# Batched matmul: y loaded four batches at a time with 24 KB runs, x transposed in blocks on VectorE, products on four row tiles

## The chip, the cores and the metric

One core of a Trainium2 chip. The metric is the device time of one execution in microseconds (us), lower is better. Each execution is marked fast or slow; for one core, slow means over 1.5% above the fastest of the same kernel. Time ratios are computed as the mean time of one kernel's fast runs over that of the other's fast runs of the same rounds, so they are not quite the ratios of the medians that are quoted beside them.

## The reference

```python
batch, dim_i, dim_j, dim_k = 32, 256, 512, 384      # x: [32,256,512], y: [32,512,384], f32
def reference(x, y):
    return np.einsum('bij,bjk->bik', x, y).astype(np.float32)
```

x is 16.8 MB, y 25.2 MB, the result 12.6 MB: 54.5 MB have to move.

## The kernel before

x comes four batches per DMA: 32 partitions a batch, 8 rows (16 KB) a partition. y comes one batch per DMA, four rows (6,144 B) on each of 128 partitions. x is transposed on the tensor engine (PE) against an identity; the copies out of PSUM, the memory that PE writes its products to, round it to f16 and write single elements 8 bytes apart, so that the columns of the later product stand in the right order. The stages of different batches are interleaved: while batch s-1 is multiplied, batch s-2 is copied out and batch s is rounded.

```python
    def transpose(q):                                   # one group of four batches
        xt_of[q] = xt_pool.tile([P, Q, NJ, NI, PQ, Q], MM_DT, name="xt_sb")
        for t in range(NJ):
            for e in range(NI):
                t_ps = tpsum_pool.tile([P, Q, Q, PQ], F32, name="t_ps")
                for h in range(Q):
                    keep(nc.tensor.transpose(t_ps[:, h]..., x_sb[:, h * NI + e, t::NJ], identity))
                dst = xt_of[q][:, :, t, e].rearrange("c g p h -> c h g p")    # 8-byte steps
                ...                                     # DVE and ACT in turn: dst <- t_ps
    # [cut: load, round_y, multiply on 128 rows, collect, store]
    for s in range(B + 2):
        if s + ahead < B: load(s + ahead)
        if s >= 2:        collect(s - 2)
        if 1 <= s <= B:   multiply(s - 1)
        if s < B and s % Q == 0: transpose(s // Q)
        if s < B:         round_y(s)
        if s >= 2:        store(s - 2)
```

## Time and profile before

| | before |
|---|---|
| time at prediction, median of 3 | 136.56 us |
| time over 6 runs, median | 136.39 us |
| profiled span | 134.7 us |
| transfers, share of the span | 97.9% |
| busiest compute engine | PE, 66% |

In the profile PE is the tensor engine, DVE is VectorE and ACT is ScalarE; PEclk is the clock that PE was granted, in tenths of full speed. The page gives, for each engine, its busy time and share of the span; then the span in 40 slices with the busy share of each in tenths; then groups of instructions with busy time, mean ns of one, and the idle time before them with what ended it.

### The profile page before, as it was taken

The numbers are of one execution on the slowest core, as the hardware profiler recorded it, in microseconds if no ns is written. First come the engines' busy times: TensorE is split into PE (matmuls) and PEld (weight loads), VectorE is DVE, ScalarE is ACT, GpSimd is POOL, SyncE is SP. The second block draws the span as 40 slices with busy tenths as digits, with TensorE's granted clock in tenths as the row PEclk, the third lists the DMA queues.
The fourth block names the chain that finished last, engine by engine and source line by source line (L and its number), as shares of the span: only waits on it lengthen the run. The fifth ranks groups of instructions, "written<-read, shape, count | busy, mean of one in ns | idle before, by whom it ended". The sixth has DMA issues, their size and how long they took to land.

```text
span 134.7 us, 1539 instructions
## 1 busy us (share of the span) xinstructions
PE 89.5 (66%) x512; PEld 66.6 (49%) x512; DVE 73.7 (55%) x128; ACT 80.1 (59%) x129; POOL 0.7 (1%) x6
## 2 busy tenths in 40 slices
PE   0049499769677908949794983949459492794920
PEld 0048368644564408925492543936259360793510
DVE  0008855975397503873489340796228870378720
ACT  3007994996299602795479650699218990179910
POOL 2000000000000000000000000000000000000000
PEclk9999999999999985686999599599995999559995
DMA  5999999999999999999999999999999999999992
GB/s 131 399 413 423 447 412 416 416 434 414 404 422 451 425 399 424 421 435 437 400 416 430 438 425 410 421 418 454 407 409 425 433 440 402 421 421 413 412 410 84
DMA packets 10375, 54.62 MB, mean 405 GB/s; under 512 B 1152, under 2 KB 1152, under 8 KB 9344
## 3 DMA queue, kind: packets, MB, share of 16 engines
q1 hardware_dynamic: 10368, 54.53, 97.9%
q8 instruction: 4, 0.07, 0.2%
q14 instruction: 3, 0.02, 0.0%
HBM read 41.94 MB, written 12.58 MB: 405 GB/s over the span
## 4 chain that ended last, share of the span: by engine, by line
DMA 79%; PE 8%; ACT 5%; DVE 2%; issue 2%; SPq 1%; DVEq 0%
DMA y_sb<-in_y_dram 30%; DMA x_sb<-in_x_dram 27%; DMA out_dram<-o_sb 21%; PE o_ps L115 4%; PE t_ps L84 4%; ACT xt_sb L94 2%; ACT y_r L102 2%; DVE xt_sb L92 1%; DVE y_r L104 1%; DVE o_sb L130 0%; SPq L69 0%; ACT o_sb L128 0%; SPq L63 0%; DVEq L130 0%
## 5 line engine op out<-in xcount | busy, mean ns | idle before, releaser
L94 ACT CAST xt_sb<-t_ps 128x512 f16<-128x512 f32 x32 | 39.8, 1350 | 44.0 <-PE t_ps L84 43.9
L92 DVE CAST xt_sb<-t_ps 128x512 f16<-128x512 f32 x32 | 40.1, 1323 | 40.3 <-PE t_ps L84 40.2
L84 PE MATMUL t_ps<-identity,x_sb 128*128 128x128 f32 x256 | 43.4, 340 | 24.5 <-DMA x_sb<-in_x_dram 24.3
L115 PE MATMUL o_ps<-y_r,xt_sb 128*128 128x384 f16 x256 | 46.3, 342 | 14.9 <-ACT y_r L102 14.9
L84 PEld LDWEIGHTS t_ps<-identity,x_sb 128*128 128x128 f32 x256 | 41.1, 216 | 27.8 <-issue 26.4
L115 PEld LDWEIGHTS <-xt_sb 128*128 128x128 f16 x256 | 26.2, 102 | 34.2 <-issue 19.9
L102 ACT CAST y_r<-y_sb 128x384 f16<-128x384 f32 x64 | 30.2, 527 | 0.6 <-DMA y_sb<-in_y_dram 0.6
L130 DVE COPY o_sb<-o_ps 128x384 f32<-128x384 f32 x32 | 17.8, 556 | 15.1 <-PE o_ps L115 15.1
L104 DVE CAST y_r<-y_sb 128x384 f16<-128x384 f32 x64 | 19.9, 354 | 0.4 <-DMA y_sb<-in_y_dram 0.4
L128 ACT COPY o_sb<-o_ps 128x384 f32<-128x384 f32 x32 | 15.4, 483 | 3.8 <-PE o_ps L115 3.8
L94 ACT ACT_TABLE_LOAD x1 | 1.3, 1283 | 0.7 <-PEq L168 0.7
masks.py:199 POOL TENSOR_SCALAR_AFFINE_SELECT identity<-identity 128x128 f32<-128x128 f32 x1 | 0.3, 294 | 0.1
masks.py:197 POOL MEMSET identity<- 128x128 f32 x1 | 0.2, 205 | 0.3 <-POOLq L168 0.3
L168 POOL MEMSET const-bfloat16-1.0<- 128x1 bf16 x1 | 0.1, 102 | 0.0
L168 POOL MEMSET const-uint8-127<- 128x1 uint8 x1 | 0.1, 102 | 0.0
L168 POOL MEMSET const-float32-0.0<- 128x1 f32 x1 | 0.1, 99 | 0.2 <-issue 0.2
L168 POOL MEMSET const-float32-1.0<- 128x1 f32 x1 | 0.1, 99 | 0.0
## 6 DMA issues: line engine op xcount, KB each, us to landing
y_sb<-in_y_dram SPq DMA_DIRECT2D x32, 768.0 KB, 15.1
x_sb<-in_x_dram SPq DMA_DIRECT2D x8, 2048.0 KB, 14.2
out_dram<-o_sb SPq DMA_DIRECT2D x32, 384.0 KB, 14.1
```

The source lines that it names most:

```text
L84: nc.tensor.transpose(t_ps[:, h].rearrange("c g p -> c (g p)"), x_sb[:, h * NI + e, t::NJ], identity,)
L92: keep(nc.vector.tensor_copy(dst, t_ps))
L94: keep(nc.scalar.copy(dst, t_ps))
L102: keep(nc.scalar.copy(yr_of[b][:, t], y_sb[:, t]))
L104: keep(nc.vector.tensor_copy(yr_of[b][:, t], y_sb[:, t]))
L115: nc.tensor.matmul(ps_of[b][e], xt_sb[:, t, e].rearrange("c p h -> c (p h)"), y_r[:, t], start=(t == 0), stop=(t == NJ - 1),)
L128: keep(nc.scalar.copy(o_of[b][:, e], ps_of[b][e]))
L130: keep(nc.vector.tensor_copy(o_of[b][:, e], ps_of[b][e]))
L168: nc = _bacc.Bacc("TRN2", target_bir_lowering=False, num_devices=1)
```

## The change

The intent is fewer and longer DMA packets: y in one load for each of the 8 groups, with runs (adjacent bytes that make one packet) of 24,576 B (the last group in two halves of 12,288 B, so 9 loads). That puts each batch on 32 partitions, so a product contracts over 32 rows, and four batches can share the 128 rows of PE as row tiles. x needs only 32x32 blocks transposed, which VectorE (DVE) does, without PE or PSUM.

```diff
-LAG = 8
+LATE = 8
+LAST = 2
+ROUND = (1, 0, 1, 1, 0, 1, 0, 1)
+    def load_y(n):
+        src = y[n * Q : (n + 1) * Q].rearrange("g (p c) k -> (g p) c k", c=C)
+        w = C // (LAST if n == N - 1 else 1)
+        for c in range(0, C, w):
+            keep(nc.sync.dma_start(out=y_of[n][:, c : c + w], in_=src[:, c : c + w]))
+    def transpose_x(n):
+        xt_of[n] = xt_pool.tile([P, C, NE, S, H], MM_DT, name="xt_sb")
+        for h in range(H):
+            rows = slice(h * NE, (h + 1) * NE)
+            keep(nc.scalar.copy(xr[:, rows], x_sb[:, rows].rearrange("q r (j c) -> q r c j", c=C)))
+            for e in range(NE):
+                keep(nc.vector.transpose(xt_of[n][:, :, e, :, h], xr[:, h * NE + e]))
+    def multiply(n, y_r):                       # all 8 PSUM banks, all end with the last c
+        ps = [[psum_pool.tile([P, K], F32, name="o_ps") for e in range(NE)] for g in range(Q)]
+        for c in range(C):
+            for e in range(NE):
+                for g in range(Q):
+                    rows = slice(g * S, (g + 1) * S)
+                    keep(nc.tensor.matmul(ps[g][e], xt_sb[rows, c, e]..., y_r[rows, c], ...))
+    for n in range(N + 1):
+        if n + 1 < N: load_y(n + 1)
+        if n + 2 < N: load_x(n + 2)
+        if n < N:
+            transpose_x(n)
+            collect(n, multiply(n, round_y(n)))
+        ...                                     # stores of the group before
 # [cut: load_x, the rounding in eight pieces (5 DVE, 3 ACT), collect, pools]
```

## The prediction

> **What bounds the kernel now.** I read the page from the top: busy shares, slices, DMA queues, groups of instructions.
>
> ```profile
> span 134.7 us, 1539 instructions
> PE 89.5 (66%) x512; PEld 66.6 (49%) x512; DVE 73.7 (55%) x128; ACT 80.1 (59%) x129; POOL 0.7 (1%) x6
> ...
> PEclk9999999999999985686999599599995999559995
> DMA  5999999999999999999999999999999999999992
> ...
> q1 hardware_dynamic: 10368, 54.53, 97.9%
> ```
>
> No compute engine is above 66%, while the DMA row is full from the second slice to the last but one: the transfers bound the kernel. 97.9% of 134.7 us is 131.9 us of transfer; only 2.8 us of start and end are not. The chain of waits agrees: 79% of it is DMA. So there are two questions: how much transfer time the change saves, and whether the compute still hides behind it.
>
> The groups give the unit costs:
>
> ```profile
> L94 ACT CAST xt_sb<-t_ps 128x512 f16<-128x512 f32 x32 | 39.8, 1350 | 44.0 <-PE t_ps L84 43.9
> L92 DVE CAST xt_sb<-t_ps 128x512 f16<-128x512 f32 x32 | 40.1, 1323 | 40.3 <-PE t_ps L84 40.2
> ...
> L102 ACT CAST y_r<-y_sb 128x384 f16<-128x384 f32 x64 | 30.2, 527 | 0.6 <-DMA y_sb<-in_y_dram 0.6
> L130 DVE COPY o_sb<-o_ps 128x384 f32<-128x384 f32 x32 | 17.8, 556 | 15.1 <-PE o_ps L115 15.1
> L104 DVE CAST y_r<-y_sb 128x384 f16<-128x384 f32 x64 | 19.9, 354 | 0.4 <-DMA y_sb<-in_y_dram 0.4
> L128 ACT COPY o_sb<-o_ps 128x384 f32<-128x384 f32 x32 | 15.4, 483 | 3.8 <-PE o_ps L115 3.8
> ```
>
> The odd ones are the first two. A 384-column copy out of PSUM takes DVE 556 ns and ACT 483 ns; 512 columns should take about 690 and 590. They take 1323 and 1350, nearly the same on two engines that otherwise differ. Reading PSUM and rounding to f16 are each cheap in the other rows; what is special is the destination: single f16 elements 8 bytes apart. That write costs about (1300-150)/512 = 2.2 ns an element on either engine.
>
> The timeline of the first batches gives back-to-back costs and the first landing:
>
> ```profile
> 8.69 4.02 PE L84 MATMUL t_ps<-identity,x_sb 128*128 128x128 f32 x20 [8.69 <-DMA x_sb<-in_x_dram]
> ...
> 15.27 1.18 DVE L104 CAST y_r<-y_sb 128x384 f16<-128x384 f32 x4
> 15.88 1.81 ACT L102 CAST y_r<-y_sb 128x384 f16<-128x384 f32 x4
> 16.51 5.36 PE L115 MATMUL o_ps<-y_r,xt_sb 128*128 128x384 f16 x32 [1.90 <-ACT y_r L102]
> ...
> 22.38 2.50 DVE L92 CAST xt_sb<-t_ps 128x512 f16<-128x512 f32 x2 [1.21 <-PE t_ps L84]
> ```
>
> x lands at 8.7 us. Thirty-two products take 5.36 us: starts 162.5 ns apart at full clock. Two of the strided copies take 2.50 us, so the second starts some 1.15 us after the first: the slow write is throughput, not latency.
>
> **What the Trainium skill says.**
> - "DMA: Bandwidth & Descriptors", section "Why small descriptors are slow", has a fixed overhead per packet. The trace agrees: its packets of 3,072, 6,144 and 16,384 B take 121, 234 and 611 ns (medians), which is 8 ns plus 27.2 B per ns.
> - "SBUF — State Buffer", section "Specifications (TRN2)", gives 16-byte lines that need at least two hits for full bandwidth. The strided copies above hit each line twice (8-byte steps) and still take 2.2 ns an element, so for these writes the measurement is worse than the page. A read with 64-byte steps, which the change adds, hits each line once; this trace has none.
> - "VectorE: DVE Perf Modes", section "The three transpose paths", gives 311 ns for a 128x128 bf16 transpose in 32x32 blocks. At one element a cycle (the 556 ns copy has 1.04 ns an element) four times the columns would be an estimated 311+400 = 0.71 us. No run here has one.
> - "TensorE: Matmul & The Clock Gate", section "Part 3: Packing small matmuls — row/col tiling", measured 3.07 times the speed for four row tiles with 512 columns. No run here shows it yet.
>
> **The change, part by part.**
>
> Transfers. y goes from 4096 packets of 6,144 B to 1024 of 24,576 B. By the fit the new one takes 8+904 = 912 ns. Over 16 engines: 4096*234/16 = 59.9 us becomes 1024*912/16 = 58.4 us, so 1.5 us less. The number of DMAs falls from 72 to 49; the 1152 four-byte completion packets of 9 ns become 784, 0.2 us less. x and out keep their packets. In all 1.7 us of 134.7, or 1.3%: the most that can be won. The transfers then take some 130.2 us, 16.3 us per group of four batches.
>
> Removed compute: 256 transposes on PE (43.4 us busy) and 64 PSUM copies (79.9 us of DVE and ACT). None of it was on the bound.
>
> Added compute, per group, eight groups:
> - ACT: 4 roundings of x, 1024 elements, contiguous writes, reads 64 bytes apart. At ACT's 0.83 ns an element plus 0.15, 1.0 us each; if the reads pay as the strided writes do, 2.4 us each.
> - DVE: 8 block transposes of 512 f16, written 8 bytes apart, the same destination stride as the 1.3 us copies. At 2.2 ns an element: 1.15 us each back to back, 9.2 us. Without that price 0.71 us, 5.7 us.
> - Rounding y in eight pieces of 768. DVE has 0.30 us per 384 back to back, plus 0.20: 0.50*5 = 2.5 us. ACT 0.45+0.32 = 0.77*3 = 2.3 us. PE can start after the first, at 0.5 us.
> - PE: 128 products of 32 rows, in 32 sets of four row tiles. With the page's 3.07, 162.5*4/3.07 = 212 ns a set, 6.8 us (estimate). PE will have been idle for the transposes, and here idle stretches are followed by half clock (0.57 and 0.60 in stretches at 49 and 60 us, records of 3.4 or 6.8 us): 3.4 us for the first 8 sets, then 24*212 = 5.1 us: 8.5 us.
> - Eight PSUM copies, four each: 1.9 us.
>
> What matters is the order. Before, the stages of different batches were interleaved on each engine, and the products had four PSUM banks beside four for transposes. Now one group takes all eight banks, every accumulator ends with the last of 16 steps, and the order of instructions shows DVE doing 8 transposes, 5 roundings, 4 copies, then the next group's transposes; ACT likewise. Those 4 copies wait for PE, so the next group's transposes wait for PE too, and PE waits for the transposes. Nothing of one group overlaps the next except transfers. The period is therefore a sum:
>
> first ACT piece and transposes, (1.0+9.2 = 10.2 us with cheap reads; 4*2.4+2.3 = 11.9 us with dear ones), about 11 us; + 0.5; + 8.5; + 1.9 = 21.9 us.
>
> That is over the 16.3 us of transfers, so the bound passes from DMA to this loop. Sum: x lands 8.7; eight periods, 175; the last stores about 3 us: span 187 us. The timed median lies 1.9 us above the profiled span (136.56 against 134.7), giving 189 us.
>
> **Rivals.**
> 1. Transposes at one element a cycle and cheap reads: 1.0+5.7+0.5+8.5+1.9 = 17.6 us. Group 0 must wait for y until about 16 us and ends at 27; 7*17.6 = 123, plus 3 and 1.9: 155 us; with PE's clock up throughout (6.8 us) about 143. For it: the page's 311 ns, and that the slow rows read PSUM, though other PSUM reads are fast. Against it: equal cost on two engines for the very stride that the transposes write.
> 2. Everything hides: period under 16.3 us, DMA stays full, the 1.7 us of packets is won, and a longer tail (one half group of products, copies and four stores after the last y) takes much of it back: 135 to 138 us. It needs cheap transposes and products near 5.4 us. For it: the careful tail (stores held back eight batches, y's last load halved) looks made for a DMA-bound kernel. Against it: the loop's sum.
> 3. Row tiles do not run side by side: 128*162.5 ns = 20.8 us on PE per group, period over 33 us, some 280 us. The different banks and the alternating row groups speak against it; I give it 3%.
>
> **Range and chances.** About 55% for the strided-write period (175 to 195 us), 25% for rival 1 (142 to 165), 15% for rival 2, the rest worse. The median of the mixture is a little below the main sum: 174 us. The range 140 to 195 us leaves rival 2 below it and rival 3 above. Faster by over 2% needs the whole packet gain and no new wait: 3%. Within 2%: 14%. Slower: 83%.
>
> **What would show it.** Right: y packets of 24,576 B near 912 ns; the DMA row no longer full, with gaps in every period; transposes of about 1.2 us each; DVE's copies and transposes waiting on PE and PE waiting on DVE in every group; PE busy in eight separate bursts, some at half clock; a period near 22 us. Transposes of 0.7 us show rival 1; a DMA row still full shows rival 2. PE bursts over 15 us would show that the row tiles don't overlap. The prediction fails most likely if the stride costs the transposes nothing or PE's bursts are much shorter than 8.5 us.

## The result, and the profile after

The changed kernel takes 179.72 us (median of 6, 179.04 to 181.38) against 136.39 us before: ratio 1.319, 95% interval 1.313 to 1.326. The transfers are no longer the bound. The page of the changed kernel, busy shares, slices and queue:

```profile
span 179.5 us, 2461 instructions
PE 60.7 (34%) x1024; PEld 31.6 (18%) x1024; DVE 108.3 (60%) x136; ACT 90.3 (50%) x89; POOL 0.2 (0%) x4
...
PEclk9999999655895559755795559755695559855696
DMA  6999999999996899939997599948999800710027
...
q1 hardware_dynamic: 7056, 54.53, 77.0%
```

No engine is near 100%, and neither is the DMA row: it has holes from the thirteenth slice on, about 54 us in. That is how a serial loop looks in this page. The groups name its parts:

```profile
L110 PE MATMUL o_ps<-y_r,xt_sb 32*128 32x384 f16 x1024 | 60.7, 409 | 112.0 <-DVE y_r L96 112.0
L87 DVE STREAM_TRANSPOSE xt_sb<-x_r 128x512 f16<-128x512 f16 x64 | 74.7, 1336 | 19.9 <-ACT x_r L85 19.9
L85 ACT CAST x_r<-x_sb 128x1024 f16<-128x1024 f32 x32 | 59.5, 1957 | 6.5 <-DMA x_sb<-in_x_dram 6.5
...
L127 DVE COPY o_sb<-o_ps 128x384 f32<-128x384 f32 x32 | 15.6, 551 | 46.5 <-PE o_ps L110 46.5
```

PE waited 112.0 us for DVE's rounding of y (which stands behind the transposes), DVE 46.5 us for PE. A transpose takes 1336 ns, as the strided copies of before did. One period, from the timeline (start and duration in us):

```profile
92.03 7.44 ACT L85 CAST x_r<-x_sb 128x1024 f16<-128x1024 f32 x4
94.00 9.33 DVE L87 STREAM_TRANSPOSE xt_sb<-x_r 128x512 f16<-128x512 f16 x8 [1.35 <-ACT x_r L85]
...
103.13 2.45 DVE L96 CAST y_r<-y_sb 128x768 f16<-128x768 f32 x5
...
103.77 7.43 PE L110 MATMUL o_ps<-y_r,xt_sb 32*128 32x384 f16 x128 [13.10 <-DVE y_r L96]
...
111.07 1.63 ACT L125 COPY o_sb<-o_ps 128x384 f32<-128x384 f32 x4 [9.41 <-PE o_ps L110]
111.23 1.95 DVE L127 COPY o_sb<-o_ps 128x384 f32<-128x384 f32 x4 [5.65 <-PE o_ps L110]
112.56 7.44 ACT L85 CAST x_r<-x_sb 128x1024 f16<-128x1024 f32 x4
```

ACT's first piece of x, 1.97 us to the first transpose; 9.33 us of transposes; the first rounding, 0.44 us to PE's start; 7.43 us of products; ACT's copies out until 112.56, when the next piece of x begins. From 92.03 to 112.56 is 20.53 us, and each of these lies after the other. The bursts of products (the 128 products of a group) start 20.5 to 21.3 us apart in all eight groups.

### The profile page after: what moved, and what is told of

Same layout as the page of the kernel before. It is cut to its first block, busy times and chain, and to the rows that moved or that the text cites. A ratio compares the mean times of both kernels' runs of the same rounds, so it can differ in the third digit from the quotient of the medians.

```text
span 179.5 us, 2461 instructions
## 1 busy us (share of the span) xinstructions
PE 60.7 (34%) x1024; PEld 31.6 (18%) x1024; DVE 108.3 (60%) x136; ACT 90.3 (50%) x89; POOL 0.2 (0%) x4
## 4 chain that ended last, share of the span: by engine, by line
DVE 35%; PE 25%; DMA 21%; ACT 11%; issue 4%; DVEq 0%; ACTq 0%
DVE xt_sb L87 33%; PE o_ps L110 25%; DMA out_dram<-o_sb 17%; ACT x_r L85 7%; DMA x_sb<-in_x_dram 4%; ACT o_sb L125 4%; DVE y_r L96 1%; DVE o_sb L127 1%; DVEq L171 0%; ACTq L85 0%; ACTq L125 0%; DVEq L127 0%
## 5 line engine op out<-in xcount | busy, mean ns | idle before, releaser
L110 PE MATMUL o_ps<-y_r,xt_sb 32*128 32x384 f16 x1024 | 60.7, 409 | 112.0 <-DVE y_r L96 112.0
L87 DVE STREAM_TRANSPOSE xt_sb<-x_r 128x512 f16<-128x512 f16 x64 | 74.7, 1336 | 19.9 <-ACT x_r L85 19.9
L85 ACT CAST x_r<-x_sb 128x1024 f16<-128x1024 f32 x32 | 59.5, 1957 | 6.5 <-DMA x_sb<-in_x_dram 6.5
L110 PEld LDWEIGHTS <-xt_sb 32*128 32x128 f16 x1024 | 31.6, 116 | 140.7 <-DVE y_r L96 94.4
L125 ACT COPY o_sb<-o_ps 128x384 f32<-128x384 f32 x32 | 13.0, 492 | 76.6 <-PE o_ps L110 76.6
L127 DVE COPY o_sb<-o_ps 128x384 f32<-128x384 f32 x32 | 15.6, 551 | 46.5 <-PE o_ps L110 46.5
L96 DVE CAST y_r<-y_sb 128x768 f16<-128x768 f32 x40 | 19.6, 562 | 0.0
L98 ACT CAST y_r<-y_sb 128x768 f16<-128x768 f32 x24 | 18.6, 861 | 0.0
```

Of the source, the lines that this page charges most:

```text
L85: keep(nc.scalar.copy(xr[:, rows], x_sb[:, rows].rearrange("q r (j c) -> q r c j", c=C)))
L87: keep(nc.vector.transpose(xt_of[n][:, :, e, :, h], xr[:, h * NE + e]))
L96: keep(nc.vector.tensor_copy(y_r[:, part], y_sb[:, part]))
L98: keep(nc.scalar.copy(y_r[:, part], y_sb[:, part]))
L110: nc.tensor.matmul(ps[g][e], xt_sb[rows, c, e].rearrange("q p h -> q (p h)"), y_r[rows, c], start=(c == 0), stop=(c == C - 1),)
L125: keep(nc.scalar.copy(o_sb[:, e], ps[g][e]))
```

## The experiments

Each kernel differs from the changed kernel by the edit shown, unless it says otherwise.

**1. Transposes that write side by side.** The result is wrong: the rows of each output block come out in another order.

```diff
-xt_pool.tile([P, C, NE, S, H], ...)   xt[:, :, e, :, h]   "q p h -> q (p h)"
+xt_pool.tile([P, C, NE, H, S], ...)   xt[:, :, e, h]      "q h p -> q (h p)"
```

> Wrong result on purpose (the rows of each output block come out in another order). The block transposes write their 32 elements side by side instead of 8 bytes apart; the weights are still 128 adjacent columns. Theory (the destination step is what makes a transpose cost 1.34 us): a transpose falls to about 0.7 us, and ACT's four copies of x of 1.86 us each with the last two transposes now set the stage, 8.8 us in place of 11.2 us; the period falls from 20.55 to about 18.1 us and the time from 179.7 to about 160 us. Rival (a block transpose of f16 costs 2.3 ns a column whatever it writes to): transposes stay at 1.34 us and the time at 180 us.

Measured: 158.69 us (ratio to before 1.164). The group of transposes in this run:

```profile
L87 DVE STREAM_TRANSPOSE xt_sb<-x_r 128x512 f16<-128x512 f16 x64 | 41.7, 690 | 31.7 <-ACT x_r L85 31.7
```

The transpose halves, 1336 to 690 ns, and the mean distance of the bursts falls from 20.73 to 17.76 us. So the slow write comes from the destination step of these 2-byte elements, not from the operation (run 7 narrows it further).

**2. The next group's transposes ahead of this group's copies.**

```diff
-            transpose_x(n)
-            collect(n, multiply(n, round_y(n)))
+            ps = multiply(n, round_y(n))
+            if n + 1 < N:
+                transpose_x(n + 1)
+            collect(n, ps)
```

> Right result. Only the order: the transposes of the next group stand ahead of the copies out of PSUM of this one, so that they run beside the products. Theory (the loop is a sum because nothing of one group overlaps the next): VectorE's own work of a group, 9.3 + 2.4 + 2.0 = 13.7 us, is under the 16.3 us of transfers, so the DMA rows fill up and the time falls to 134 to 139 us. Rival (the engines themselves are too slow, or the slow writes hold the products up when they run together): the time stays above 150 us.

Measured: right result, 143.17 us (ratio 1.049), above the expected 134 to 139. Busy time of the engines in single periods, first of the changed kernel, then of this one (columns: stretch, its length, PE, weight loads, DVE, ACT, POOL, granted clock, DMA share, GB/s):

```profile
83.20:103.80 20.60, 7.50 (x132) 3.88 (x136) 13.53 (x18) 11.13 (x11) 0.00 (x0) 0.67 0.87 331
103.80:124.30 20.50, 7.41 (x128) 3.81 (x128) 13.50 (x18) 11.12 (x11) 0.00 (x0) 0.67 0.85 330
```

```profile
77.90:94.20 16.30, 8.15 (x128) 3.99 (x128) 13.47 (x18) 11.25 (x11) 0.00 (x0) 0.71 1.01 411
94.20:111.20 17.00, 6.87 (x132) 3.63 (x136) 13.47 (x18) 11.24 (x11) 0.00 (x0) 0.70 1.01 422
124.00:141.40 17.40, 7.43 (x128) 3.74 (x128) 6.94 (x14) 3.19 (x6) 0.00 (x0) 0.70 0.55 218
```

DVE works 13.5 us a group in both. In the serial order a period is 20.5 us; in this order it is 16.3 to 17.0 us with the DMA share at 1.01: bound by transfers. A reordering with not one instruction less gives back 36.5 of the 43.3 us, so the serial order is shown to be the main cause. Shortening the sum instead, by cheaper transposes, gives back 21.0 us in run 1 and 27.0 us in run 7; these gains overlap and do not add up. The last stretch shows what is left: in the tail the transfers work 55% of the time.

**3. ACT reads x in the order in which it lies.** Its output is wrong, which doesn't matter for the time.

```diff
-x_sb[:, rows].rearrange("q r (j c) -> q r c j", c=C)
+x_sb[:, rows].rearrange("q r (c j) -> q r c j", c=C)
```

> Wrong result on purpose. ACT reads x in the order in which it lies instead of 64 bytes apart; it writes the same. Theory (the reads of 64-byte step double ACT's copy, and only the first copy of each group lies on the path): the copy falls from 1.96 us to about 1.0 us, the period by 0.9 us, the time by some 7 us to 172 us; the transposes stay at 1.34 us. Rival (ACT's copies bound the stage): the time falls by three or four copies a group, 25 us or more. Rival (reads cost nothing, the copy is slow for another reason): 180 us.

```profile
L85 ACT CAST x_r<-x_sb 128x1024 f16<-128x1024 f32 x32 | 31.3, 1071 | 6.6 <-DMA x_sb<-in_x_dram 6.6
```

The copy fell to 1071 ns as expected, but the time only to 178.79 us (ratio 1.310; 1.319 for the changed kernel in its own rounds). The 7 us did not come. In this trace the bursts are 8.26 to 8.29 us long in the later groups, 7.4 in the changed kernel, so the other work of a period did fall, from 13.1 to 12.2 us, and the burst took it back. The records of granted clock say how. In the changed kernel a burst began at 103.77 us and full clock came at 107.99, 4.2 us later; here one began at 100.30 and full clock came at 106.20, 5.9 us later. The records are multiples of 3.413 us. The Trainium skill ("TensorE: Matmul & The Clock Gate", section "Part 1: The HAM clock gate (the "warmup" mystery)") describes a free-running window of 3413 ns in which PE's activity decides the clock, and the trace agrees. In this reading, a burst that starts at a worse place in the windows runs longer at half clock; run 9 puts a form of it to the test.

**4. Deeper buffers.** Three for x and y, loads one group further ahead.

> Right result. Three buffers for x and for y in place of two, and the loads one group further ahead; the order on the compute engines is the same. Theory (the loop of the engines bounds, the transfers wait for it): same time within 1%, 178 to 181 us. Rival (two buffers are too few, the holes in the DMA row are what costs): the holes close and the time falls below 165 us.

Measured: 178.31 and 180.74 us in the two fast executions (181.0 and 181.47 us in the two marked slow), ratio 1.317: unchanged. The holes in the DMA row are a consequence. In this trace the loads run ahead, the DMA row stays full through the 27th slice, and the holes move to the end.

**5 and 6. Transfers alone**, y with runs of 6,144 B and of 24,576 B. Both store zeros and do no compute but one fill. The diff is between the two, in words.

```diff
 for each group: load x (16 KB runs)
-    four times: load y of a batch (6,144 B), store a batch
+    load y of four batches (24,576 B); four times: store a batch
```

> Wrong result on purpose: only the transfers of the kernel before (x in 8, y in 32 with runs of 6,144 B, out in 32, zeros stored), no compute but one fill. If the kernel before is bound by its transfers, this takes about as long as it: 132 us of packets and 2 to 3 us of start and end, 134 to 137 us. If the compute costs it anything, this is clearly shorter.

> Wrong result on purpose: the same transfers with y in 8 loads with runs of 24,576 B. By the 8 ns of a packet, 1.7 us less than with runs of 6,144 B (1.3%); nothing else changes. Rival (longer packets move no faster, or hold others up): no difference or slower.

Measured on the same chip: 135.61 us with short runs (ratio to the kernel before 0.995, interval 0.993 to 0.997), 136.60 us with long ones (1.002, 0.999 to 1.004). The first shows that the kernel before was at its transfers' own time within 0.5%. The second was expected 1.7 us below the first and is 1.0 us above it. Length is not all that differs between the two: with short runs the four y loads of a group alternate with stores, with long runs one y load stands ahead of four stores. The queue lines of the two traces, in the same order:

```profile
q1 hardware_dynamic: 10368, 54.53, 98.5%
```

```profile
q1 hardware_dynamic: 6912, 54.53, 97.2%
```

97.2% of 135.3 us is 131.5 us of packets; 98.5% of 133.9 us is 131.9 us. The saving has shrunk to 0.4 us, because more packets of x and y took over a tenth longer than their kind's median (by summing the excess over all: 2.6 us of 16 engines in place of 1.2). And the 16 engines ended less evenly: with long runs 10.6 of them were active in the microsecond from 131 us, then 4.6, 1.9 and 0.1; with short runs 9.5 and 0.2. That is one profile of each; in run 12 the end is uneven with short runs too (below). Why single packets are slow was not tested and stays open.

**7. Pairs of f16 transposed as 4-byte elements.** Right result. ACT writes two rows of x side by side, DVE transposes 512 elements of 4 bytes, also 8 bytes apart.

```diff
-for e in range(NE): nc.vector.transpose(xt[:, :, e, :, h], xr[:, h * NE + e])          # 8 a group
+for e in range(NE): nc.vector.transpose(xt.bitcast(F32)[:, :, e, :, hh], xr.bitcast(F32)[:, hh, e]...)   # 4 a group
```

> Right result, if the transpose passes bits through. Two rows of x stand side by side as f16 pairs and are transposed as one 4-byte element: 4 transposes of 512 elements a group in place of 8, each element written 8 bytes from the last. If each separate write costs 2.3 ns whatever its width, a transpose stays at 1.3 us and the four take 5.3 us in place of 10.7; if only a 2-byte element 8 bytes apart is slow, it falls to 0.7 us. Either way ACT's four copies (7.4 us) now set the stage: 7.4 + 0.7 to 1.3 us in place of 11.2, period 18 us, time 158 to 164 us. If nothing of this holds, 180 us.

Measured: 152.71 us (ratio 1.119), below the expected 158 to 164.

```profile
L88 DVE STREAM_TRANSPOSE xt_sb<-x_r 128x512 f32<-128x512 f32 x32 | 22.8, 712 | 46.5 <-ACT x_r L86 46.5
```

The same number of writes, the same 8-byte step, and 712 in place of 1336 ns: it is the 2-byte element 8 bytes apart that is slow, not the step alone. Other steps of 2-byte elements were not run. The bursts stand 17.06 us apart, 1 us less than I had reckoned, which over eight groups is about the shortfall.

**8. The pipelined order with stores held back by twelve batches** (16 output buffers), the second experiment's kernel otherwise.

> Right result. The pipelined order of the second experiment, stores held back by twelve batches in place of eight (16 output buffers), so that the last y is loaded 3.8 us of transfers earlier and more stores are left to run beside the last products. Theory (after the pipelining the rest of the loss is the tail: transfers are full until the last y and then idle for some 5 us): 138 to 140 us. Rival (the loss lies in the loop, in slower packets): 143 us as before.

Measured: 138.03 and 139.03 us in the two fast executions (140.25 and 140.60 us in the two marked slow), ratio 1.015. Of the 4.9% that the second experiment had left, 3.4 points are gone: by the fast executions the tail was some two thirds of it.

**9. One fill of DVE more on the serial path.**

```diff
             transpose_x(n)
+            keep(nc.vector.memset(idle, 0.0))
             collect(n, multiply(n, round_y(n)))
```

> Right result. One more VectorE instruction a group, a fill of about 0.95 us between the transposes and the first rounding of y, on the path of the serial loop. Theory of the sum: the period grows by 0.95 us, eight times: 187 us. Theory of the clock windows (the period sits at 20.48 us, six records of 3.413 us, because a burst of products that begins later spends less of itself at half clock): the period stays at 20.4 to 20.5 us, the burst shortens from 7.4 to about 6.5 us, the time stays within 1.5 us of 179.7 us.

Measured: 186.31 us (ratio 1.368). The fill itself took 0.78 us, and the work of a period beside the burst grew from 13.1 to 14.0 us. The sum had said 187 us, and is right; the clock windows as I had put them fall: the distances of the bursts go 20.72, 22.29, 21.41, 20.97, 20.71, 22.27, 21.39 us and the bursts 6.7 to 8.3 us. What the windows can give is limited. Over the traces of the changed kernel and of runs 3, 4 and 9 the bursts lie between 6.7 and 8.3 us, and full clock comes 2.7 to 6.0 us after a burst starts. With 12.2 us of other work (run 3) or 13.1 (changed kernel) a burst of 8.3 or 7.4 us fits a period of 20.48 us, six windows; with 14.0 us (this run) it would have to be 6.5 us, which none is, and the period moves on. That fits all four traces, but was put together after them, and no run was made to test it. Two kept traces that it was not made from agree: run 7 (10.04 us of other work, bursts of 7.03 us) stands at 17.06 us, five windows; run 1 (10.55 us) would need a burst of 6.5 us for five windows, and its bursts go round from 8.3 to 6.7 us with distances of 17.3 to 18.9 us. So a saving on the path can be given back by the burst, as in run 3.

**10. PE kept busy during the transposes**, by 64 products that are thrown away.

> Right result. 64 products of no use on 128 rows run on PE while the block transposes run (into a bank that the first real product clears), so that PE's clock is up when the real burst begins. If half clock costs 2.2 us of each period, the burst falls from 7.4 to about 5.3 us and the period from 20.5 to about 18.4 us; time about 163 us. If the clock is not what lengthens the burst, 180 us or more.

Measured: 176.22 us (ratio 1.294), a gain of 3.5 us in place of 17. Timeline of one period:

```profile
107.93 10.56 PE L109 MATMUL o_ps<-y_r,xt_sb 128*128 128x384 f16 x64 [0.38 <-ACT o_sb L138]
...
120.72 7.06 PE L123 MATMUL o_ps<-y_r,xt_sb 32*128 32x384 f16 x128 [2.23 <-DVE y_r L96]
```

The useless products end at 118.49 us; 2.23 us of idle follow, and the clock went to half at 121.44 us for 3.41 us, in the middle of the burst. So it went in six of the seven groups that have useless products. The seventh escaped it, although its idle gap (2.22 us) was as long; so the length of the gap alone does not decide. Its burst took 5.38 us and its period was 18.54 us, as the expectation had it for all (5.3 and 18.4). So the clock's share of a burst is seen, in one group only.

**11 and 12. All that helped together** (pipelined order, pairs, stores held back by sixteen batches), with y in runs of 24,576 B and, in the twelfth, in four loads a group with runs of 6,144 B.

> Right result. All that helped together: the pipelined order, pair transposes, stores held back by sixteen batches with 20 output buffers. Theory (what is left is the tail): transfers run full to the end, 132.5 us of packets and 3 us of start and end: 136 to 138.5 us, no faster than the kernel before by 2%. If the gain of the long packets came through, 133.5 to 135 us.

> Right result. As the run before it, but each group's y comes in four loads of four rows a partition, with runs of 6,144 B. If the long runs are worth their 1.5 us of packet overhead, this is 1.5 us slower than the run with 24,576 B; if long packets give that back through slower packets and uneven ends of the 16 engines, it is as fast or faster.

Measured on the same chip: 138.24 us (ratio 1.014, interval 1.012 to 1.016) and 139.47 us (1.026, 1.023 to 1.028). The page of the eleventh run:

```profile
DMA  5999999999999999999999999999999999999970
...
q1 hardware_dynamic: 7056, 54.53, 96.1%
```

The transfers are full to the end, yet 1.4% slower than before. Packets take 96.1% of 137.0 us, 131.7 us, and before 131.9 us: of the 1.7 us to be saved 0.2 us are left. The long y packets themselves take 912 ns (median) as reckoned, but those of x take 637 ns in the mean against 627 before, and the last half loads and the stores are a little slower too. And the engines end unevenly, 10.2 of 16 active from 132 us, then 4.7, 2.0 and 0.4. In run 12, with y in short runs, they end as unevenly (13.5 from 133 us, then 9.0, 5.1 and 1.1), so the uneven end is not shown to come from long runs. Here the long runs are worth 1.2 us against the short ones, the opposite of runs 5 and 6; which of the two a kernel gets stays open. No version with a right result beats the kernel before.

## Why the prediction was right

- **The bound moves from the transfers to a serial loop.** Right: the DMA share fell from 97.9 to 77.0%, and run 2 undid most of the loss by order alone. Gaps in the DMA row were foretold for every period; they begin only some 54 us in.
- **The strided write costs the transposes 1.15 us each, back to back.** Right: 9.33 us for eight (predicted 9.2), 0.69 us without the step (estimated 0.71). The estimates' 1.04 ns an element for DVE and 0.83 for ACT do not quite come out of the trace: with the 0.15 us by which two strided copies overlapped, the 384-column copies give 1.06 and 0.87. No cost changes by more than 0.05 us.
- **ACT's copies of x**, left between 1.0 and 2.4 us: 1.96 us. With the first of them the stage is 11.3 us (about 11 predicted).
- **The burst of products**, 8.5 us: mis-sized, 7.4 us. I took 212 ns for a set of four row tiles from the skill's factor of 3.07. In the later part of a burst four products start within 8 ns of each other, and the next four 162 ns after them: the full factor of 4. Half clock lasted 4.2 us, not 3.4.
- **Copies out**, 1.9 us: 1.4 us from the burst's end to ACT's next piece of x count, since ACT's own four set it, not DVE's.
- **The sum**, 21.9 us a period and 189 us: 20.5 us and 179.7 us. Of the 1.4 us the burst is 1.1, the copies out are 0.5, and the first stage took 0.3 us more. The end after the last copy took 4.8 us, not 3. The point of 174 us was 3% low, and does not follow from its own chances: they put 40% at or below 165 us and the next 55% between 175 and 195, so the median lies above 175 us. The range of 140 to 195 us took in rival 1 as well; that the time fell inside it says little, and the terms of the sum are what was tested.
- **The transfers' gain of 1.7 us.** Each packet of 24,576 B takes 912 ns as worked out, but the gain that should follow is not there in the transfers alone (run 6), where more packets are slow and the engines end unevenly. This step was not borne out there (runs 11 and 12 show 1.2 us of it); it was hidden behind the loop and did not touch the time.
- **Rival 1** (cheap transposes) and **rival 2** (all hidden) are out by the 1336 ns and by the holes in the DMA row. **Rival 3** (no overlap of row tiles) is out by 7.4 us for 128 products.

## What to carry to other kernels

When a change makes the stages of one group depend on each other and takes all buffers of one kind (here all eight PSUM banks), write down the order of instructions on each engine and add the stages up before looking at busy shares: a period can be half again as long as the busiest engine's work. Before trading a copy for another with the same destination, look at what that destination cost. And a gain per packet is to be measured, to the end of the slowest DMA engine, with the transfers alone and in the kernel: here the two disagreed.

## What the Trainium skill lacked or had wrong

- "SBUF — State Buffer": two hits on a 16-byte line are said to be enough. f16 elements written 8 bytes apart cost DVE 1336 ns per 512 in a transpose against 690 side by side, while 4-byte elements at the same step took 712 ns.
- "SBUF — State Buffer": the penalty for a new line at each access has no figure for ScalarE. Reads of f32 with 64-byte steps took 1957 ns per 1024 elements, adjacent ones 1071 ns.
- "TensorE: Matmul & The Clock Gate": four row tiles are given a factor of 3.07 with 512 columns. With 384 columns and four PSUM banks, sets of four at full clock stood 162 ns apart, the same as single products before (162.5 ns): a factor of 4 (512 columns were not run).
- "TensorE: Matmul & The Clock Gate": it warns of PE gaps of more than about 3.4 us. In run 10 gaps of 2.2 us were followed by 3.41 us at half clock in six of seven groups (and in the seventh not).
- "DMA: Bandwidth & Descriptors": the fixed cost per packet is there (8 ns here), but not that fewer, longer packets may not shorten a stream: 136.6 us with 24,576 B against 135.6 us with 6,144 B, with the transfers alone (in the whole kernel, runs 11 and 12, the long runs were 1.2 us faster).
